# The MLP's pool of inner halves moves from the right side of SBUF to the left

## The chip, the cores and the metric

The kernel runs on one core of a Trainium2 chip. The metric is device time in microseconds (us), from the start of the program to the end of its last instruction; every time below is of that kind. A core has five engines that work side by side and are held together by semaphores: TensorE (PE, matrix products), VectorE (DVE), ScalarE (ACT), GpSimd (POOL) and SyncE (SP, which here issues most loads). SBUF is the on-chip memory of 128 partitions, and all addresses below are bytes in one partition.

## The reference, cut to what matters

The function is an encoder trunk of two layers over a sequence of 512 with 1024 channels. Each layer is a mixer and an MLP, both behind a norm whose shift, scale and gate come from the conditioning vector c. Layer 0 mixes with convolution and retention, layer 1 with S5 and a GLU:

```python
for layer in range(DEPTH):
    mod = (c_act @ ada_w[layer] + ada_b[layer])[:, None, :]
    shift_m, scale_m, gate_m, shift_f, scale_f, gate_f = jnp.split(mod, 6, axis=-1)
    h = _rmsnorm(x, norm_g[layer, 0]) * (1.0 + scale_m) + shift_m
    ...
    x = x + gate_m * mix
    h = _rmsnorm(x, norm_g[layer, 1]) * (1.0 + scale_f) + shift_f
    x = x + gate_f * (jnp.square(jax.nn.relu(h @ w_fc1[layer])) @ w_fc2[layer])
return _rmsnorm(x, norm_f)
```

## The kernel before

Activations lie with channels on partitions, as eight tiles of 128x512. Every large product is computed in three matmuls: an operand is split into a high part (a cast on ScalarE) and a low part (a subtraction on VectorE), and hi*hi, hi*lo and lo*hi are added up in PSUM (`mm3`). A weight unit of 128x1024 is loaded into a `raw` tile (7 slots, shared by all streams of weights, those of the modulation included), cast to `wh` (L197) and subtracted to `wl` (L192). A unit is then eight times three matmuls of 128x512 into one PSUM tile.

The program runs through `mixer0`, `mlp(0)`, `s5` (which ends with the GLU), `mlp(1)` and the final norm. At the end of `mixer0` the eight output units of `w_out` give the new x tiles (L719), their squares are summed (L284 on VectorE), the first inputs `fh` and `fl` of the MLP are formed (L753, L754), and background work runs beside it: `silu_c` loads c into `cb` and applies silu (L420, L421), and `ada_dve` computes four modulation columns on VectorE from loaded `raw<-adt` units (L436, sixteen of them). Then `mlp(0)` starts on the not yet normalised inputs with two fc1 units (`wl_2200` and `wl_2204` are their low parts) and applies the norm's factor later; `raw<-fc` are the MLP's weights, `ident,rr` is the broadcast of that factor.

Beside `mlp(0)`, VectorE and GpSimd build the matrices of S5 and write them to DRAM. At the entry to `s5` the first of them are loaded back in this order: `wi`, `cs`, then a GLU weight (`raw<-w_ga`), `tt`, `e`, and again `wi`, `cs`, `tt`, `e` for the second block.

Tiles come from pools. Pools of the left side of SBUF are stacked upwards, pools of the right side downwards from the top (229344). The pool `fp` holds the MLP's inner halves: eight slots of `fh` and eight of `fl`, 2048 bytes each, 32768 in all. It is opened by `open_fp` at the end of `mixer0` and again at the end of `s5`, and closed after each MLP. A tile that is put where another lay waits until the last reader or writer of the old one is done.

The scheduler arranges the instructions of each engine itself, from its own estimate of when operands and places come free; matmuls of some stretches and all loads of SyncE (`load`, L175) are kept in the order of the program.

Of the kernel before, what the change touches and what calls it, by code (L numbers as in the profile page):

```python
# [135 lines left out]
class Kern:  # L136
# [602 lines left out]

    def open_fp(self):  # L740
        self.fp = self.stack.enter_context(
            self.tc.tile_pool(name="fp", bufs=8, side="right", reuse_waits="tile"))


    def pre(self, l, i):
# [959 lines left out]
```

## Time and profile before

| what | value |
|---|---|
| three runs | 1225.39, 1228.76, 1229.54 us |
| their median | 1228.76 us |
| the profiled execution | 1225.63 us, of which the span is 1223.9 us |
| mean granted TensorE clock | 0.985 |
| busy share of the span | PE 96%, DVE 71%, ACT 39% |

The span runs from the first to the last instruction in the trace; the rest of the profiled execution's time (1.7 us) lies around it. Shares are means over all stages. At the ends of the stages VectorE or a load can be what the next instruction waits for.

### The profile page before, as it was taken

The numbers are of one execution on the slowest core, as the hardware profiler recorded it, in microseconds if no ns is written. First come the engines' busy times: TensorE is split into PE (matmuls) and PEld (weight loads), VectorE is DVE, ScalarE is ACT, GpSimd is POOL, SyncE is SP. The second block draws the span as 40 slices with busy tenths as digits, with TensorE's granted clock in tenths as the row PEclk, the third lists the DMA queues.
The fourth block names the chain that finished last, engine by engine and source line by source line (L and its number), as shares of the span: only waits on it lengthen the run. The fifth ranks groups of instructions, "written<-read, shape, count | busy, mean of one in ns | idle before, by whom it ended". The sixth has DMA issues, their size and how long they took to land.

```text
span 1223.9 us, 17714 instructions
## 1 busy us (share of the span) xinstructions
PE 1175.5 (96%) x6830; PEld 932.9 (76%) x6830; DVE 873.4 (71%) x1605; ACT 475.9 (39%) x752; POOL 109.4 (9%) x223
## 2 busy tenths in 40 slices
PE   6999999999999999999989888999999999999996
PEld 5777756776878878878767677788888888888885
DVE  6899995899998799798968999498552332332343
ACT  4423313455523423423424674344551532422530
POOL 0000000100011223344422100000000000000000
PEclk9999999999999999999999898999999999999998
DMA  9755341635356689889798877376343332333201
GB/s 354 259 172 184 132 170 35 213 118 189 104 159 233 212 285 290 262 282 277 216 337 291 310 265 284 121 244 212 147 138 103 88 102 86 103 90 100 69 1 69
DMA packets 65700, 223.59 MB, mean 183 GB/s; under 512 B 11168, under 2 KB 11552, under 8 KB 63568
## 3 DMA queue, kind: packets, MB, share of 16 engines
q1 hardware_dynamic: 48528, 174.63, 42.0%
q0 software_dynamic: 16512, 46.79, 12.5%
q8 instruction: 53, 0.87, 0.3%
q10 hardware_dynamic: 576, 1.05, 0.2%
q14 instruction: 31, 0.25, 0.1%
HBM read 197.77 MB, written 29.82 MB: 186 GB/s over the span
## 4 chain that ended last, share of the span: by engine, by line
PE 83%; DVE 8%; DMA 5%; ACT 2%; issue 1%; SPq 0%; DVEq 0%; ACTq 0%
PE ps L170 83%; DVE wk L1296 2%; DMA wk<-k_chan 1%; DMA raw<-adn 1%; DVE xt L1428 1%; DMA raw<-adt 1%; DVE xt L1427 1%; PE ps L1252 1%; DVE wl L192 0%; DMA raw<-fc 0%; DMA x<-x 0%; DVE hx L1296 0%; DVE wk L1684 0%; ACT wh L197 0%; DVE sr L1296 0%
## 5 line engine op out<-in xcount | busy, mean ns | idle before, releaser
L197 ACT CAST wh<-raw 128x1024 fp32r<-128x1024 f32 x169 | 176.6, 1050 | 515.1 <-PE ps L170 452.7
L192 DVE TENSOR_TENSOR wl<-raw,wh 128x1024 fp32r<-128x1024 f32 x169 | 205.9, 1222 | 179.1 <-ACT wh L197 177.3
L170 PE MATMUL ps<-hh,wh 128*128 128x512 f32 x808 | 317.5, 399 | 4.6 <-ACT cm L789 2.2
L170 PE MATMUL ps<-hl,wh 128*128 128x512 f32 x808 | 317.1, 393 | 1.6 <-DVE hl L238 1.2
L170 PE MATMUL ps<-hh,wl 128*128 128x512 f32 x808 | 316.3, 392 | 0.8 <-DVE wl L192 0.8
L170 PE MATMUL ps<-fl,wh 128*128 128x512 f32 x544 | 215.9, 398 | 1.4 <-DVE fl L811 1.4
L170 PE MATMUL ps<-fh,wh 128*128 128x512 f32 x544 | 216.9, 400 | 0.0
L170 PE MATMUL ps<-fh,wl 128*128 128x512 f32 x544 | 216.0, 398 | 0.0
L170 PEld LDWEIGHTS ps<-hh,wh 128*128 128x128 f32 x808 | 152.4, 189 | 43.7 <-ACT wh L197 3.5
L170 PEld LDWEIGHTS ps<-hh,wl 128*128 128x128 f32 x808 | 152.7, 189 | 33.8 <-DVE wl L192 1.2
L170 PEld LDWEIGHTS ps<-hl,wh 128*128 128x128 f32 x808 | 152.8, 189 | 33.6 <-DVE hl L238 1.6
L170 PEld LDWEIGHTS ps<-fl,wh 128*128 128x128 f32 x544 | 102.9, 189 | 26.1 <-DVE fl L811 1.9
L170 PEld LDWEIGHTS ps<-fh,wh 128*128 128x128 f32 x544 | 102.8, 189 | 25.2 <-issue 0.8
L170 PEld LDWEIGHTS ps<-fh,wl 128*128 128x128 f32 x544 | 102.7, 189 | 24.8
L538 DVE SCALAR_TENSOR_TENSOR cacc<-apad,cvw,cacc 128x512 f32<-128x512 f32 x120 | 83.6, 744 | 0.0
L827 DVE SCALAR_TENSOR_TENSOR x<-ps,mod,x 128x512 f32<-128x512 f32 x40 | 29.9, 748 | 68.2 <-PE ps L170 68.1
L811 DVE TENSOR_TENSOR fl<-wk,fh 128x512 fp32r<-128x512 f32 x64 | 44.0, 688 | 18.1 <-ACT fh L810 18.1
L862 DVE TENSOR_TENSOR w<-pb,bt 128x512 f32<-128x512 f32 x64 | 41.4, 686 | 5.0 <-DMA bt<-bt 2.8
L280 ACT ACTIVATE wk<-x 128x512 f32<-128x512 f32 x35 | 22.1, 631 | 58.2 <-DVE x L827 32.7
L807 ACT ACTIVATE wk<-wk 128x512 f32<-128x512 f32 x64 | 40.7, 636 | 1.5
L810 ACT CAST fh<-wk 128x512 fp32r<-128x512 f32 x64 | 39.8, 622 | 1.7
L436 DVE SCALAR_TENSOR_TENSOR raw<-raw,x 128x512 f32<-128x512 f32 x52 | 33.2, 686 | 9.2 <-DMA raw<-adt 6.8
(245 smaller groups left out, 1285.8 us busy)
## 6 DMA issues: line engine op xcount, KB each, us to landing
raw<-fc SPq DMA_DIRECT2D x128, 512.0 KB, 4.3
raw<-adn SPq DMA_DIRECT2D x50, 512.0 KB, 4.9
raw<-adt SPq DMA_DIRECT2D x34, 512.0 KB, 4.9
pb<-d_pw POOLq DMA_DIRECT2D x32, 256.0 KB, 8.5
bt<-bt POOLq DMA_DIRECT2D x16, 512.0 KB, 9.6
d_e<-eb POOLq DMA_DIRECT2D x16, 512.0 KB, 4.7
d_wi<-eb POOLq DMA_DIRECT2D x16, 512.0 KB, 7.8
wi<-d_wi SPq DMA_DIRECT2D x8, 1024.0 KB, 5.7
```

The source lines that it names most:

```text
L170: i = self.nc.tensor.matmul(out, lhsT=lhsT, rhs=rhs, start=start, stop=stop, **kw)
L192: self.keep(self.nc.vector.tensor_tensor(lo, raw, hi.bitcast(F32), SUB))
L197: self.keep(self.nc.scalar.copy(hi, raw))
L280: nc.scalar.activation(sq, t, AF.Square)
L436: self.keep(nc.vector.scalar_tensor_tensor(half, half, 1.0, self.cb[k], MUL, MUL, accum_out=v[:, 2 * k + h:2 * k + h + 1]))
L538: nc.vector.scalar_tensor_tensor(ac, ap[:, t:t + S], cvw[:, i * TAPS + t:i * TAPS + t + 1], ac, MUL, ADD)
L807: nc.scalar.activation(f, r, AF.Square)
L810: nc.scalar.copy(hi, f)
L811: nc.vector.tensor_tensor(lo, f, hi.bitcast(F32), SUB)
L827: nc.vector.scalar_tensor_tensor(self.x[m], ps, gate[:, m:m + 1], self.x[m], MUL, ADD)
L862: V.tensor_tensor(o, x, y, op)
L1296: pin(nc.vector.tensor_tensor(*args))
```

## The change

The pool `fp` is allocated from the left side.

```diff
     def open_fp(self):
         self.fp = self.stack.enter_context(
-            self.tc.tile_pool(name="fp", bufs=8, side="right", reuse_waits="tile"))
+            self.tc.tile_pool(name="fp", bufs=8, reuse_waits="tile"))
```

Before, `fp` lay at 196576 to 229344, above everything else; after, it lies at 155104 to 187872, directly on the pools that live all the time, and the pools that are opened after it (`cb`, and `pl` for the work beside the MLP) start at 187872 instead of 155104 and end at 229344. In `s5`, which opens its pool when `fp` is closed, both slots of `wi` (155104 to 171488) and those of `cs` and `tt` then lie where the MLP's `fh` and `fl` were, and `e` lies where the background work was; before, these four lay on the background work and the second slot of `e` on `fh`.

The program's operations are the same, but the scheduler arranges the end of `mixer0` otherwise. VectorE, at the first new x tile (`x_1945`), before: all sixteen L436 of the modulation (on `raw_1975` to `raw_2067`) stand ahead of it.

```order
L438 TENSOR_TENSOR rv_2070<-rv_2070 128x2
L382 TENSOR_TENSOR mod_123<-rv_2070,adab_122 128x2
L719 SCALAR_TENSOR_TENSOR x_1945<-ps_1790,mod_123,x_104 128x64x8
L719 SCALAR_TENSOR_TENSOR x_1966<-ps_1791,mod_123,x_106 128x64x8
L866 TENSOR_SCALAR s1_2416<-s8_2423 128x64
L719 SCALAR_TENSOR_TENSOR x_1979<-ps_1792,mod_123,x_108 128x64x8
L192 TENSOR_TENSOR wl_1782<-raw_1772,wh_1780 128x1024
L719 SCALAR_TENSOR_TENSOR x_1999<-ps_1793,mod_123,x_110 128x64x8
L866 TENSOR_SCALAR s2_2417<-s1_2416 128x64
L192 TENSOR_TENSOR wl_1788<-raw_1778,wh_1786 128x1024
L192 TENSOR_TENSOR wl_2023<-raw_1784,wh_2021 128x1024
L754 SCALAR_TENSOR_TENSOR fl_1950<-x_1945,gs_124,fh_1949 128x512
```

The same place after the change:

```order
L436 SCALAR_TENSOR_TENSOR raw_1995,rv_2008<-raw_1995,cb0_1956 128x512
L436 SCALAR_TENSOR_TENSOR raw_1995,rv_2008<-raw_1995,cb1_1957 128x512
L719 SCALAR_TENSOR_TENSOR x_1945<-ps_1790,mod_123,x_104 128x64x8
L436 SCALAR_TENSOR_TENSOR raw_1996,rv_2008<-raw_1996,cb0_1956 128x512
L719 SCALAR_TENSOR_TENSOR x_1966<-ps_1791,mod_123,x_106 128x64x8
L436 SCALAR_TENSOR_TENSOR raw_1996,rv_2008<-raw_1996,cb1_1957 128x512
L866 TENSOR_SCALAR s1_2416<-s8_2423 128x64
L192 TENSOR_TENSOR wl_1782<-raw_1772,wh_1780 128x1024
L719 SCALAR_TENSOR_TENSOR x_1979<-ps_1792,mod_123,x_108 128x64x8
L192 TENSOR_TENSOR wl_1788<-raw_1778,wh_1786 128x1024
L436 SCALAR_TENSOR_TENSOR raw_2015,rv_2059<-raw_2015,cb0_1956 128x512
L436 SCALAR_TENSOR_TENSOR raw_2015,rv_2059<-raw_2015,cb1_1957 128x512
```

Six L436 stand ahead of `x_1945` now, and ten come after it, between the x tiles and the low parts of the units. The multiplications of the retention's gates (L704) and `cb` have changed places as well: the gates are first, so `cb` and the modulation start later.

VectorE, some twenty rows further on, at the low part `wl_2200` of the first fc1 unit, before:

```order
L284 TENSOR_TENSOR ssq_1947<-ssq_1947,wk_1968 128x512
L754 SCALAR_TENSOR_TENSOR fl_1972<-x_1966,gs_124,fh_1971 128x512
L754 SCALAR_TENSOR_TENSOR fl_1985<-x_1979,gs_124,fh_1984 128x512
L870 SCALAR_TENSOR_TENSOR s1_2416<-s2_2417,s1_2416 128x64
L754 SCALAR_TENSOR_TENSOR fl_2005<-x_1999,gs_124,fh_2004 128x512
L719 SCALAR_TENSOR_TENSOR x_2050<-ps_2025,mod_123,x_112 128x64x8
L284 TENSOR_TENSOR ssq_1947<-ssq_1947,wk_1981 128x512
L192 TENSOR_TENSOR wl_2200<-raw_2194,wh_2198 128x1024
L870 SCALAR_TENSOR_TENSOR s1_2416<-s2_2417,s1_2416 128x64
```

After:

```order
L719 SCALAR_TENSOR_TENSOR x_2148<-ps_2123,mod_123,x_116 128x64x8
L438 TENSOR_TENSOR rv_2070<-rv_2070 128x2
L870 SCALAR_TENSOR_TENSOR s1_2416<-s2_2417,s1_2416 128x64
L284 TENSOR_TENSOR ssq_1947<-ssq_1947,wk_2052 128x512
L382 TENSOR_TENSOR mod_123<-rv_2070,adab_122 128x2
L866 TENSOR_SCALAR s3_2418<-s1_2416 128x64
L866 TENSOR_SCALAR s2_2417<-s2_2417 128x64
L284 TENSOR_TENSOR ssq_1947<-ssq_1947,wk_2116 128x512
L192 TENSOR_TENSOR wl_2200<-raw_2194,wh_2198 128x1024
```

Before, `wl_2200` came right after the fifth x tile (`x_2050`) and the second sum of squares (L284); now the seventh x tile (`x_2148`) and the fifth sum of squares stand ahead of it. From `x_1945` up to and with `wl_2200` VectorE has, after the change, 46 instructions: 7 L719, 10 L436, 5 L192, 6 L754, 5 L284 and 13 small ones of 64 columns or fewer. The slot of `raw` into which the first fc1 unit is loaded comes free with `wl_1788` before and with `wl_2087` after (the row 349 of VectorE, 21 of the 46); that of the second with `wl_2023` before and after with the second L436 on `raw_2066` (30 of the 46). TensorE takes the last products of the four open output units one unit after the other instead of all four high parts first, so that three matmuls fewer stand ahead of the end of the first; and it takes nineteen matmuls of the first fc1 unit before the second unit's first, where it took three.

SyncE, at the entry to `s5`, with the semaphores that each load waits for, before:

```order
L177 DMA wi_6051<-d_wi_132 128x2048 [waits DMASW7_49,DMASW5_49,DVE_49]
L177 DMA cs_6053<-d_tab_129 128x1024 [waits DMASW4_49,DMASW5_49,DMASW3_49,DMASW6_49,DMASW2_49,DMASW7_49,DMASW1_49,DMAHW1_49,DMASW0_49,Pool_49]
L177 DMA raw_6055<-w_ga 128x1024 [waits DMAHW5_49,DMAHW2_49,Activation_49]
L177 DMA tt_6057<-d_t_134 128x1024 [waits DMASW7_49,DMAHW3_49,DMASW0_49,Pool_49]
L177 DMA e_6059<-d_e_131 128x2048 [waits DMASW3_49,DMASW4_49,DMASW2_49,DMASW7_49,DMASW1_49,DMAHW4_49,DMASW0_49,PE_49]
```

After:

```order
L177 DMA wi_6051<-d_wi_132 128x2048 [waits DMASW5_49,DMASW7_49,PE_49,Pool_49]
L177 DMA cs_6053<-d_tab_129 128x1024 [waits DMAHW1_49,DMASW4_49]
L177 DMA raw_6055<-w_ga 128x1024 [waits DMAHW5_49,DMAHW2_49,DVE_49]
L177 DMA tt_6057<-d_t_134 128x1024 [waits DMASW5_49,DMASW6_49,DMASW3_49,DMASW7_49,DMASW2_49,DMAHW3_49,DMASW1_49,DMASW0_49]
L177 DMA e_6059<-d_e_131 128x2048 [waits DMAHW4_49,DVE_49]
```

The order is the same. `wi` waits for a matmul now (PE_49) where it waited for VectorE, and the semaphore's value is that of the last matmul of `mlp(0)`, which reads `fh_5575` and `wl_5897`; `e` waits for VectorE where it waited for that matmul. The loads in between have no wait for TensorE, but stand behind `wi` in SyncE's order. From there to the end the order of every engine is unchanged.

## Rows read from the trace of the kernel before

**Rows 1.** The page of the profile: busy time of each engine, and the chain by line.

```profile
PE 1175.5 (96%) x6830; PEld 932.9 (76%) x6830; DVE 873.4 (71%) x1605; ACT 475.9 (39%) x752; POOL 109.4 (9%) x223
...
PE ps L170 83%; DVE wk L1296 2%; DMA wk<-k_chan 1%; DMA raw<-adn 1%; DVE xt L1428 1%; DMA raw<-adt 1%; DVE xt L1427 1%; PE ps L1252 1%; DVE wl L192 0%; DMA raw<-fc 0%; DMA x<-x 0%; DVE hx L1296 0%; DVE wk L1684 0%; ACT wh L197 0%; DVE sr L1296 0%
```

**Rows 2.** VectorE's timeline, 226 to 260 us (start, duration, operation, idle before).

```profile
226.70 0.68 DVE L436 SCALAR_TENSOR_TENSOR raw<-raw,cb 128x512 f32<-128x512 f32 x1
...
227.31 0.69 DVE L436 SCALAR_TENSOR_TENSOR raw<-raw,cb 128x512 f32<-128x512 f32 x1
...
244.21 2.13 DVE L719 SCALAR_TENSOR_TENSOR x<-ps,mod,x 128x512 f32<-128x512 f32 x2 [1.73 <-PE ps L170]
...
247.22 1.22 DVE L192 TENSOR_TENSOR wl<-raw,wh 128x1024 fp32r<-128x1024 f32 x1
...
254.20 1.41 DVE L754 SCALAR_TENSOR_TENSOR fl<-x,gs,fh 128x512 fp32r<-128x512 f32 x2
255.53 0.22 DVE L870 SCALAR_TENSOR_TENSOR s<-s,s 128x64 f32<-128x64 f32 x1
...
256.32 1.14 DVE L719 SCALAR_TENSOR_TENSOR x<-ps,mod,x 128x512 f32<-128x512 f32 x1
257.30 0.68 DVE L284 TENSOR_TENSOR ssq<-ssq,wk 128x512 f32<-128x512 f32 x1
257.90 1.21 DVE L192 TENSOR_TENSOR wl<-raw,wh 128x1024 fp32r<-128x1024 f32 x1
259.03 0.22 DVE L870 SCALAR_TENSOR_TENSOR s<-s,s 128x64 f32<-128x64 f32 x1
```

**Rows 3.** TensorE's timeline at the same place: first unit, first MLP matmuls, broadcast.

```profile
248.50 0.50 PE L170 MATMUL ps<-hh,wl 128*128 128x512 f32 x1 [0.78 <-DVE wl L192]
...
269.02 0.40 PE L170 MATMUL ps<-fh,wh 128*128 128x512 f32 x1
...
269.48 0.39 PE L170 MATMUL ps<-fh,wl 128*128 128x512 f32 x1
...
282.04 1.05 PE L170 MATMUL ps<-ident,rr 128*128 128x128 f32 x8
```

**Rows 4.** Loads into raw tiles, 215 to 300 us: time to landing.

```profile
DMA to landing us min/median/max: 3.6/4.5/9.1
```

**Rows 5.** SyncE's timeline, 640 to 680 us: the S5 loads.

```profile
658.20 0.33 SPq L177 DMA_DIRECT2D wi<-d_wi  x1
...
659.33 0.36 SPq L177 DMA_DIRECT2D raw<-w_ga  x1
```

**Rows 6.** Timelines of TensorE, ScalarE and VectorE at the entry to S5.

```profile
663.78 0.40 PE L170 MATMUL ps<-fh,wl 128*128 128x512 f32 x1
...
671.39 3.51 PE L170 MATMUL ps<-hl,wi 128*64 128x64 f32 x64 [0.46 <-DVE hl L1296]
...
684.30 0.44 PE L170 MATMUL ps<-tt,hl 128*64 128x128 f32 x4
...
669.00 1.05 ACT L197 CAST wh<-raw 128x1024 fp32r<-128x1024 f32 x1
...
672.05 1.22 DVE L192 TENSOR_TENSOR wl<-raw,wh 128x1024 fp32r<-128x1024 f32 x1
...
674.94 1.29 DVE L1296 TENSOR_TENSOR wk<-ps,cs 128x512 f32<-128x512 f32 x2 [0.42 <-PE ps L170]
```

**Rows 7.** Landings of all wi loads; then of w_ga alone, issued at 659.33.

```profile
DMA to landing us min/median/max: 4.7/5.7/11.1
...
DMA to landing us min/median/max: 8.9/8.9/8.9
```

**Rows 8.** Stretches: PE, PEld, DVE, ACT, POOL busy; clock, DMA share, GB/s.

```profile
664.00:760.00 96.00, 80.40 (x1113) 65.96 (x1113) 92.08 (x138) 61.87 (x162) 5.60 (x10) 0.93 0.84 313
...
668.00:670.00 2.00, 0.97 (x18) 0.46 (x8) 1.81 (x8) 1.51 (x4) 0.79 (x2) 1.00 1.08 440
```

**Rows 9.** Busy time in the stretch after the k_chan load is awaited.

```profile
605.00:640.00 35.00, 30.47 (x197) 23.63 (x196) 23.63 (x43) 8.95 (x13) 9.38 (x18) 0.97 0.97 327
```

## The prediction, made before the changed kernel ran

> **What bounds the kernel now.** I read the page first: TensorE is busy for 96% of the span, and in the chain its matmuls hold 83%, with small shares for VectorE (S5's products, L1296) and for a load of `k_chan` [rows 1]. So a change that moves only places and waits can show only where TensorE waits now, or where the change makes it wait. Two such places are touched, and I read them from the timelines. At the end of `mixer0` TensorE waits 0.78 us for the low part `wl_1782` of an output unit before the matmul at 248.50, then has no gap worth a row up to the first MLP matmul at 269.02 [rows 3]. VectorE feeds it there: it sits idle for 1.73 us until `x_1945` can start at 244.21, and works without a gap from there [rows 2]. At the entry to S5 the roles turn: from 664 to 760 us VectorE is busy for 92.08 of 96 us and TensorE for 80.40 [rows 8], so there whatever delays VectorE delays the end.
>
> **The change part by part: the end of the mixer.** The reader has seen that ten L436 are moved from VectorE's idle time ahead of `x_1945` to the loaded stretch behind it, and that `wl_2200`, which the third MLP matmul needs, is now the 46th instruction from `x_1945`. I price the 46 by the distance from one start to the next: L719 0.98 (256.32 to 257.30), L284 0.60 (to 257.90), L192 1.13 (to 259.03), L436 0.61 (226.70 to 227.31), L754 0.665 (two in the 1.33 from 254.20 to 255.53), and a small one 0.125 (255.53 to 256.32 holds one and an L754) [rows 2]. That is 7 x 0.98 + 10 x 0.61 + 5 x 1.13 + 6 x 0.665 + 5 x 0.60 + 13 x 0.125 = 27.2 us.
>
> The start: three matmuls of some 0.23 us fewer (269.02 to 269.48 holds two [rows 3]) stand ahead of the first x tile, so `x_1945` starts at 244.21 - 0.68 = 243.53. `wl_2200` is then done at 270.8, and its matmul can start 0.06 later (as 248.50 follows the end of `wl_1782`, 247.22 + 1.22 = 248.44 [rows 2, 3]), at 270.9.
>
> When does TensorE come to it? The six instructions up to `wl_1782` take 2 x 0.98 + 2 x 0.61 + 0.125 + 1.22 = 4.5 us, so it is done at 248.06 and TensorE goes on at 248.12, 0.38 us earlier than before. The work from there is the same, so the third MLP matmul is reached at 269.48 - 0.38 = 269.10 [rows 3]. It waits 1.8 us, and against before it starts 1.4 us late. Nothing behind it gives that back: in the 13 us from 269.02 to the broadcast at 282.04 [rows 3] TensorE is the bound, and the MLP behind goes on by TensorE. **Term: +1.4 us.** Bounds: if VectorE gains 1.8 us on this count, there is no wait and -0.4 us remains; if each instruction took its whole duration, with no overlap (7 x 1.14 + 10 x 0.69 + 5 x 1.21 + 6 x 0.705 + 5 x 0.68 + 13 x 0.22 = 31.4 us [rows 2]), `wl_2200` would come at 275.0, +5.5 us. The starts in a row show the overlap, so I take the first count.
>
> The loads are moved too. The load of the first fc1 unit waited for the second low part after `x_1945`; now its slot comes free after 21 of the 46, by the same distances 15.1 us, at 258.7. It lands 4.5 us later by the median, 9.1 by the slowest here [rows 4], at 263.2 or 267.8, and with the cast (1.05 us, as the one at 669.00 [rows 6]) at 268.9 at the latest. `wl_2200` starts at about 269.6, so VectorE's queue covers it; without that cover it would cost what it comes late. The second unit's load comes free after 30 of the 46, at 263.4, and lands at 267.9 to 272.5; TensorE wants its high part only after nineteen matmuls of the first unit (some 4.2 us), at 274.8. Both are priced at nothing.
>
> **The entry to S5.** `wi` was issued at 658.20, under the MLP's last matmuls [rows 5]; now it waits for the last of them, which starts at 663.78 and takes 0.40 [rows 6]: 664.2, 6.0 us later. Behind it on SyncE stand `cs`, `w_ga`, `tt` and `e`. `wi` itself lands 4.7 to 5.7 us after its issue (fastest and median of eight [rows 7]), 668.9 to 669.9, and TensorE needs it at 671.39 [rows 6], when its other operand comes: no cost, unless it takes the longest landing of the eight, 11.1.
>
> `w_ga` has less room. It was issued 1.13 us after `wi` and landed 8.9 us later, at 668.2 [rows 5, 7]; the cast was at 669.00, and VectorE took the low part at 672.05 [rows 6]. Now it is issued at 665.3. Upper bound of its landing: the same 8.9 us, 674.2. Lower bound: `wi` at its fastest, 668.9, and then the 1 MB of `cs` and `w_ga` at the 440 GB/s that the queues move at 668 us [rows 8], 2.4 us: 671.3. I take 672.3, nearer the lower bound, since the loads before had to share with the background's last writes. With the cast, VectorE starts `wl` at 673.4 instead of 672.05, 1.3 us late, and 0.42 us of that lies in its later wait for TensorE, ahead of 674.94 [rows 6]. **Term: +0.9 us**, with bounds of 0 (a landing at 671.3 makes it 0.3 late, which that wait takes up) and +2.8 (674.2). What waits behind the instruction at 672.05 is VectorE's whole queue of S5, and TensorE with it.
>
> The Trainium skill, "DMA: Bandwidth & Descriptors", section "Rules for kernel authors", says to issue a DMA early, compute, and wait for its semaphore late. This trace agrees: `w_ga` landed at 668.2, 0.8 us ahead of its cast, only because it left before the MLP's end. The rule speaks against the change, which puts the issue at that end.
>
> `tt` is not wanted before 684.30 [rows 6]: issued half a us behind `w_ga`, at 665.8, it is there by 676.9 even with the longest landing of rows 7, 11.1; `e` and the second block's loads are wanted later still. At MLP 1 the second `fp` finds its place free. All are priced at nothing.
>
> **The sum.** 1.4 + 0.9 = +2.3 us. The profiled execution took 1225.63 us, so it would be 1227.9. That execution is 3.1 us below the median of the three runs, 1228.76; I put the base midway, 1227.2, and predict 1229.5 us. A measurement of this kernel tells some 0.3%, 3.7 us, from no change; so the forecast is: a small loss that reads as no change.
>
> **The rivals.**
> *A, slower: S5's entry pays in full.* `w_ga` keeps its 8.9 us, the loads behind it now being issued together with it: +2.8, sum +4.2, 1231.4 us. It passes 0.3% if `w_ga` lands after 673.7. For it: that the queues are full at 440 GB/s [rows 8]; against: less background traffic. Chance 0.18.
> *B, slower: VectorE's queue ahead of `wl_2200` slips* towards its whole durations: +5.5 + 0.9, 1233.6 us. It decides from a `wl_2200` ready after 272.3. Against it: the measured starts. Chance 0.07.
> *C, faster: the wait for `k_chan`.* From 605 to 640 us TensorE is busy for 30.47 of 35 us [rows 9], behind a load that MLP 0's background awaits. The shift of TensorE against the background could shorten it; all of it back would be -4.5 + 2.3, 1225.0 us, and with both terms at their lower ends 1222.3. Against it: that chain's order is unchanged. Chance 0.11.
> *D, nothing.* VectorE catches up and `w_ga` lands by 671.3: 1226.8 to 1227.2 us. For it: the lower bounds. Chance 0.16. The same page of the Trainium skill, section "Anatomy of one DMA", gives 2.0 us and the bytes by 436 GB/s; as an estimate the 2 MB up to `w_ga` would be there at 671.0, which goes with this rival.
> My forecast has 0.48.
>
> **Range and chances.** Taking off half of C below and half of B above, and with the 1.5 us by which the base is uncertain, 1223.0 to 1235.5 us; the likeliest case alone, 1227 to 1232. Faster by over 0.3%: only C at its lower end or with a low base, 0.10. Slower: B, most of A, and a little of the forecast, 0.25. Within 0.3%: 0.65.
>
> **What would show it.** First, a TensorE wait of one to two us for VectorE (L192) at the third MLP matmul, near 270, and the broadcast near 283.4; a wait under 0.3 us there makes the first term wrong. Second, `wi` issued right after the MLP's last matmul, `w_ga` landing near 672 to 673 measured from a last matmul at 664 (both shifted by the first term), and VectorE's `wl` waiting for ScalarE's cast; if `wl` waits for nothing, the second term is 0. Third, no change in the time from there to the end. The prediction is wrong if a stretch that neither place touches changes by more than 2 us, above all 605 to 640, or if `wi` itself holds TensorE.

## The result, and the profile after

The changed kernel took 1235.01 us (median of 10 runs, 1231.22 to 1244.67) against 1227.57 us before on the same chip (10 runs, 1223.51 to 1229.54): a ratio of 1.0071, 95% interval 1.0046 to 1.0096. It is slower by 0.7%. 1229.5 us had been predicted, within 1223.0 to 1235.5, and "no change" as the likeliest reading.

The page of the profile after (span 1231.3 us, profiled execution 1233.1 us), first the busy times, then the chain of waits by line:

```profile
PE 1175.3 (95%) x6830; PEld 933.5 (76%) x6830; DVE 873.5 (71%) x1605; ACT 475.8 (39%) x752; POOL 109.5 (9%) x223
...
PE ps L170 83%; DMA raw<-fc 2%; DMA raw<-adn 1%; DMA raw<-adt 1%; DMA wi<-d_wi 1%; DVE wl L192 1%; PE ps L1252 1%; DMA hh<-adn 1%; DVE raw L436 1%; DVE x L719 0%; DVE w L862 0%; DMA x<-x 0%; PE ps L1341 0%; DVE wk L1684 0%; ACT tu L1363 0%
```

The busy times are those of before [rows 1] within 0.2 us for each engine (TensorE's weight loads within 0.6); the span is 7.4 us longer. So no engine has more to do, and TensorE stands idle for 7.6 us more (1231.3 - 1175.3 us against 1223.9 - 1175.5). Sums over the whole span do not tell where. I looked for it by comparing when the same event comes in both traces.

**The end of the mixer.** VectorE's timeline after (start, duration, operation, idle time before it and what ended it):

```profile
228.68 0.69 DVE L704 TENSOR_TENSOR g<-g,ps 128x512 f32<-128x512 f32 x1 [7.32 <-PE ps L170]
...
235.29 0.69 DVE L421 TENSOR_TENSOR cb<-cb,wk 128x512 f32<-128x512 f32 x1 [1.25 <-ACT wk L420]
...
242.96 1.17 DVE L719 SCALAR_TENSOR_TENSOR x<-ps,mod,x 128x512 f32<-128x512 f32 x1 [2.21 <-PE ps L170]
```

The first row is the one to look at. VectorE sits idle for 7.32 us until the first gate's product comes from TensorE. Before, `cb` and the L436 [rows 2] filled this time; now the gates (L704) stand first in VectorE's order and `cb` behind them, though its load was there. The stretch 216 to 245 us (busy times of PE, PEld, DVE, ACT, POOL; granted clock, DMA share, GB/s), before and after:

```profile
216.00:245.00 29.00, 27.43 (x151) 22.80 (x144) 25.08 (x70) 11.30 (x18) 3.10 (x10) 1.00 0.72 228
...
216.00:245.00 29.00, 27.85 (x133) 23.22 (x133) 17.71 (x43) 10.46 (x15) 0.00 (x0) 0.94 0.31 113
```

VectorE sits idle for 7.4 us more (11.29 against 3.92). Not all of it is the order's: in this profile TensorE's granted clock was 0.91 from 209.00 to 227.59 us, between two of its broadcasts, where it was 1.00 before, and TensorE took 1.6 us longer there. The run with less background (below) keeps the changed order and had the clock at 1.00 there; in it VectorE is idle for 9.7 us. What the order leaves over is work: from the first L669 (212.25 before, 210.09 after) to `x_1945` VectorE is busy for 28.04 us before and 21.57 after, so 6.5 us, the ten L436 above all, are not yet done. Then TensorE's timeline. Before, the stretch begins with this broadcast:

```profile
228.16 3.73 PE L170 MATMUL ps<-ident,rr 128*128 128x128 f32 x32
```

And after:

```profile
227.59 3.73 PE L170 MATMUL ps<-ident,rr 128*128 128x128 f32 x32
...
269.95 0.50 PE L170 MATMUL ps<-fh,wl 128*128 128x512 f32 x1 [1.22 <-DVE wl L192]
...
282.60 1.05 PE L170 MATMUL ps<-ident,rr 128*128 128x128 f32 x8
```

This answers to [rows 3]: the third MLP matmul waits for VectorE. Counted from the broadcast at 228.16 or 227.59, `x_1945` comes 0.68 us earlier (15.37 us behind it instead of 16.05), the third matmul 1.0 us later (42.36 instead of 41.32) and the MLP's broadcast 1.1 us later; in the trace's own time that broadcast comes 0.56 us later than before. From there TensorE catches up: at 348 us it is 0.3 us ahead of before.

**Eighty us later.** TensorE's timeline in the middle of MLP 0, where the background of S5 has its transposes (L1089, of the phases `wd`). First before, where TensorE comes to them without a wait:

```profile
360.66 1.03 PE L1089 MATMUL ps<-ident,wd 128*128 128x128 f32 x8
361.45 0.48 PE L170 MATMUL ps<-fh,wh 128*128 128x512 f32 x1
361.76 0.40 PE L170 MATMUL ps<-fl,wh 128*128 128x512 f32 x1
362.00 0.40 PE L170 MATMUL ps<-fh,wl 128*128 128x512 f32 x1
362.23 0.39 PE L170 MATMUL ps<-fh,wh 128*128 128x512 f32 x1
```

And after:

```profile
362.68 1.12 PE L1089 MATMUL ps<-ident,wd 128*128 128x128 f32 x4 [2.19 <-DVE wd L874]
365.04 1.12 PE L1089 MATMUL ps<-ident,wd 128*128 128x128 f32 x4 [1.24 <-DVE wd L874]
...
366.81 0.63 PE L170 MATMUL ps<-fh,wl 128*128 128x512 f32 x1
367.24 0.63 PE L170 MATMUL ps<-fh,wh 128*128 128x512 f32 x1
```

Two things are to be read. TensorE waits 2.19 + 1.24 = 3.43 us for VectorE's copies of the phases (L874). And the matmuls behind the wait start 0.43 us apart (366.81 to 367.24), where they start some 0.235 apart before (362.00 to 362.23). VectorE's timeline says why. The last copies before:

```profile
354.98 1.93 DVE L874 COPY wd<-wd 64x512 f32<-64x512 f32 x3
```

And after:

```profile
363.80 1.19 DVE L874 COPY wd<-wd 64x512 f32<-64x512 f32 x2
```

They end at 356.9 and at 365.0, which is 74.9 and 82.4 us after the broadcast, 7.5 us later. From the broadcast to the last copy, before and after (columns as above):

```profile
282.04:356.91 74.87, 72.26 (x397) 56.63 (x396) 69.97 (x203) 37.47 (x56) 0.00 (x0) 1.00 0.48 162
...
282.60:364.99 82.39, 76.82 (x417) 60.26 (x415) 76.66 (x234) 38.40 (x57) 0.00 (x0) 0.98 0.47 154
```

So 6.7 of the 7.5 us are work of VectorE: what is left of the work not done at the mixer's end, and two low parts of weights more (15 L192 instead of 13, 2.6 us), which TensorE's units want before the late copies are done. Before, TensorE came to the transposes 3.8 us behind the last copy (360.66 against 356.9); that was all the slack there was. The stretch 360 to 370 us (columns as above), before:

```profile
360.00:370.00 10.00, 10.00 (x49) 8.16 (x48) 7.77 (x11) 3.07 (x4) 6.30 (x12) 1.00 0.71 238
```

And after:

```profile
360.00:370.00 10.00, 6.57 (x22) 4.90 (x21) 9.70 (x18) 2.22 (x3) 2.18 (x4) 0.66 0.30 96
```

The granted clock is 0.66 of full speed after the wait, 1.00 before: part of the stretch ran at 1.2 GHz and not at 2.4. Between 348 and 384 us TensorE goes from 0.3 us ahead to 5.9 us late: 6.2 us, of which 3.4 are the wait and 2.8 the lower clock. It stays 5.9 us late up to 505 us.

**The rest.** Near 524 and 530 us TensorE waits 1.66 and 1.08 us for `fl` (L811), where the first profile of before shows one wait of 0.77: 2.2 us with what lies around them. The end of MLP 0 comes 7.95 us late. At the entry to S5 three timelines answer to [rows 5, 6]. SyncE's:

```profile
672.22 0.33 SPq L177 DMA_DIRECT2D wi<-d_wi  x1
```

ScalarE's:

```profile
680.37 1.04 ACT L197 CAST wh<-raw 128x1024 fp32r<-128x1024 f32 x1 [3.31 <-DMA raw<-w_ga]
```

And VectorE's:

```profile
681.45 1.23 DVE L192 TENSOR_TENSOR wl<-raw,wh 128x1024 fp32r<-128x1024 f32 x1 [1.36 <-ACT wh L197]
```

`wi` is issued 0.09 us after the end of the MLP's last matmul (671.74 + 0.39), ScalarE waits for `w_ga`, and VectorE for ScalarE. The first scan of S5 starts 8.84 us later than before, 0.89 more than MLP 0's end. Behind it TensorE waits for the second block's `wi`, for which it does not wait before:

```profile
689.26 3.02 PE L170 MATMUL ps<-hl,wi 128*64 128x64 f32 x64 [3.90 <-DMA wi<-d_wi]
```

That wait costs nothing here, since VectorE works on: all 32 scans come between 8.84 and 8.86 us late. At the end of S5 1.4 us come back: before, TensorE ran at a granted clock of 0.83 from 760 to 770 us; after, the same part of the program (768 to 778 us) ran at 1.00. From the end of S5 to the end of the program both traces take 438.55 us. The end is 7.4 us late: -0.3 + 6.2 + 2.2 - 0.2 + 0.9 - 1.4.

### The profile page after: what moved, and what is told of

Its sections match the earlier page's. It is cut to its first block, busy times and chain, and to the rows that moved or that the text cites. A ratio compares the mean times of both kernels' runs of the same rounds, so it can differ in the third digit from the quotient of the medians.

```text
span 1231.3 us, 17715 instructions
## 1 busy us (share of the span) xinstructions
PE 1175.3 (95%) x6830; PEld 933.5 (76%) x6830; DVE 873.5 (71%) x1605; ACT 475.8 (39%) x752; POOL 109.5 (9%) x223
## 4 chain that ended last, share of the span: by engine, by line
PE 84%; DMA 7%; DVE 5%; ACT 2%; issue 2%; SPq 0%; DVEq 0%; ACTq 0%
PE ps L170 83%; DMA raw<-fc 2%; DMA raw<-adn 1%; DMA raw<-adt 1%; DMA wi<-d_wi 1%; DVE wl L192 1%; PE ps L1252 1%; DMA hh<-adn 1%; DVE raw L436 1%; DVE x L719 0%; DVE w L862 0%; DMA x<-x 0%; PE ps L1341 0%; DVE wk L1684 0%; ACT tu L1363 0%
## 5 line engine op out<-in xcount | busy, mean ns | idle before, releaser
L192 DVE TENSOR_TENSOR wl<-raw,wh 128x1024 fp32r<-128x1024 f32 x169 | 206.1, 1221 | 178.7 <-ACT wh L197 176.7
L811 DVE TENSOR_TENSOR fl<-wk,fh 128x512 fp32r<-128x512 f32 x64 | 43.9, 688 | 19.7 <-ACT fh L810 19.7
L436 DVE SCALAR_TENSOR_TENSOR raw<-raw,x 128x512 f32<-128x512 f32 x52 | 33.3, 686 | 11.8 <-DMA raw<-adt 11.8
```

The costliest lines, as they stand in the source:

```text
L192: self.keep(self.nc.vector.tensor_tensor(lo, raw, hi.bitcast(F32), SUB))
L436: self.keep(nc.vector.scalar_tensor_tensor(half, half, 1.0, self.cb[k], MUL, MUL, accum_out=v[:, 2 * k + h:2 * k + h + 1]))
L811: nc.vector.tensor_tensor(lo, f, hi.bitcast(F32), SUB)
```

## The experiments

Theory one: the order at the mixer's end costs VectorE idle time, and this comes out as a wait at L1089 and a low clock behind it. Rivals: the new places as such (S5's loads, MLP 1); and, theory two, that the lateness of the background meets TensorE anywhere, L1089 being only the first place. Ratios are against the kernel before on the same chip, with their 95% intervals.

**Only layer 1 on the left.** `fp` stays right for MLP 0 and goes left for MLP 1.

```diff
-            self.open_fp()
+            self.open_fp(side="right")
...
```

(`open_fp` hands the side on to the pool.)

> The pool is left on the right side for layer 0's MLP and goes to the left only for layer 1's; the order of TensorE, VectorE and SyncE is that of before. If the loss comes from what the pool's place in layer 0 does to the order at the end of the mixer (and to the S5 loads), the time is that of before within 0.3%, and no wait over 0.5 us stands at the phase transposes (L1089). If the place of the pool itself is slow (its addresses, read by the MLP's matmuls), layer 1's MLP takes about as much longer as layer 0's did, and some 3 to 4 us of the 7.4 show here.

Measured: 1225.82 us, ratio 0.9995 (0.9980 to 1.0011); no wait at L1089. The place in MLP 1 costs nothing that shows.

**Only the order at the mixer's end.** The kernel before, `fp` on the right, with a gap that puts `cb` at 187872, where it lies after the change.

```diff
-                    cb = dp.enter_context(tc.tile_pool(name="cb", bufs=1, reuse_waits="tile"))
+                    cb = dp.enter_context(tc.tile_pool(name="cb", bufs=1, reuse_waits="tile")); cb.tile([P, 8192], F32, name="gap")
```

> The kernel before, with the MLP's pool on the right, and only the pool of c moved up by 32768 bytes, to 187872, where the change put it; S5's loads keep their places. The scheduler then puts the gates ahead of c and ten L436 behind the first x tile, as after the change. If the order is the cause, VectorE is idle for some 10 us between 221 and 244, the phase copies come 7 to 8 us later, TensorE waits 2 to 4 us at L1089, and the time is 1232 to 1236 us, with wi issued under the MLP's last matmuls as before. If the loss lies in S5's loads or in the pool's place, the time is that of before, 1226 to 1229.

Measured: 1238.1 us, ratio 1.0080 (1.0047 to 1.0112). VectorE's timeline:

```profile
230.10 0.69 DVE L704 TENSOR_TENSOR g<-g,ps 128x512 f32<-128x512 f32 x1 [5.72 <-PE ps L170]
```

TensorE's:

```profile
367.20 2.35 PE L1089 MATMUL ps<-ident,wd 128*128 128x128 f32 x8 [5.46 <-DVE wd L874]
```

The stretches there, columns as above:

```profile
360.00:370.00 10.00, 4.42 (x18) 3.25 (x17) 9.44 (x20) 2.04 (x3) 0.00 (x0) 0.83 0.28 93
370.00:380.00 10.00, 10.00 (x37) 7.93 (x37) 9.70 (x15) 1.23 (x2) 6.46 (x12) 0.82 0.44 159
```

The gap alone gives the idle time, the wait and a loss as large as the change's, while the way from MLP 0's end to the first scan stays at 13.45 us (13.33 before, 14.22 after). So it is the order that the scheduler makes when `cb` lies there, and neither `fp`'s side itself nor, but for its 0.9 us, S5. This order is not in every row that of the change: the third MLP matmul does not wait here, and the wait at L1089 is longer.

**The transposes one block later**, on the changed kernel, to take TensorE's wait away and leave VectorE's lateness.

```diff
-                if b == 0:
+                if b == 1:
                     turns()
```

> The changed kernel, with the transposes of the phases (L1089) put one table block later in the program (a block is 2.4 us or more of VectorE's work), so that TensorE comes to them later. If VectorE's backlog meets TensorE there, the wait of 3.4 us and the low clock behind it go for the most part, and the time falls by 3 to 6 us, to 1229 to 1232. If the later wait at 524 to 530 us is a consequence of the same backlog, it goes or stays independently of this, and is read from the trace: under 1.0 us if TensorE's delay at L1089 was its cause, 2 to 3 us if VectorE's backlog or the loads were. If the order at the mixer's end costs by itself, the time stays at 1235.

Measured: 1237.46 us, ratio 1.0077 (1.0051 to 1.0103). The wait at L1089 is gone, and nothing is gained. TensorE's timeline shows what came in its place (the granted clock was 0.83 from 420 to 430 us):

```profile
422.65 0.50 PE L170 MATMUL ps<-fh,wh 128*128 128x512 f32 x1 [1.62 <-ACT wh L197]
423.91 0.51 PE L170 MATMUL ps<-fh,wl 128*128 128x512 f32 x1 [0.52 <-DVE wl L192]
...
647.29 0.66 PE L1252 MATMUL ps<-eb,bp 128*32 128x128 f32 x8 [2.85 <-DVE eb L862]
```

From the broadcast to the end of MLP 0 it takes 391.85 us (after: 389.37, before: 381.98). This speaks for theory two: to move one meeting point does not remove the lateness.

**The GLU's weight first**, on the changed kernel: `w_ga` is issued ahead of `wi`.

```diff
+            self.glu.ahead(4, 3)
             load(0, "wi", "cs")
...
-            self.glu.ahead(4, 3)
```

> The changed kernel, with the GLU weight w_ga loaded ahead of wi and cs at the entry to S5, so that it doesn't stand behind the load that waits for the MLP's last matmul. By the theory of the prediction VectorE's low part no longer waits for the cast, and the first scan starts 0.9 us earlier against the MLP's last matmul (13.3 us behind it, as before, instead of 14.2). If the end of S5 is set by VectorE, the total falls by 0.9 us; if by TensorE's clock in the last blocks, it does not move by more than 0.5. In no case does it give back the 6 to 8 us that arise ahead of S5.

Measured: 1235.35 us, ratio 1.0083 (1.0057 to 1.0109); from MLP 0's end to the first scan 14.21 us (14.22 without the edit). The load came early (issued at 660.49), but then its cast stands ahead of the norm's L258 in ScalarE's timeline:

```profile
677.68 1.03 ACT L197 CAST wh<-raw 128x1024 fp32r<-128x1024 f32 x1
678.62 0.20 ACT L258 ACTIVATE rt<-rv 128x4 f32<-128x4 f32 x1
```

VectorE then waits 1.43 us for `rt`, 0.95 more than after the change alone (0.48), and after that no more for the cast (1.36 there). One wait was changed into another.

**Doses of VectorE work at the mixer's end**, on the kernel before: five or ten multiplications of 128x512 (0.69 us each) on a work tile, in its old order.

```diff
             ts(lr, lr, -1e-4, None, ALU.min)
+            nc.vector.memset(w1, 0.0)
+            for _ in range(5):
+                V.tensor_tensor(w1, w1, w1, MUL)
```

> The kernel before, with VectorE given a memset and five more multiplications of 128x512 (0.60 us each, some 3.3 us in all) on a scratch tile that the phases' computation writes later; they lie between the x tiles at the end of the mixer, ahead of the phases, and the output does not depend on them. Theory one, a slack at the transposes: before the change the phase copies are ready 3.8 us ahead of TensorE (356.9 against 360.66), so this dose causes no wait at L1089 and the time is that of before within 0.3%. Theory two, the work beside the MLP is itself the longest path up to S5 (TensorE waits for its end, 2.44 and 1.50 us at 636 to 638): whatever delays it comes through one for one, here +3 us, as a longer wait at 636 or at an earlier place.

> The same with ten multiplications, 6.3 us in all, about the VectorE time that the change loses ahead of the first x tile. Theory one: a wait of some 2.5 us at L1089 with 2 us of low clock behind it, +4 to +5 us. Theory two: +6 us, wherever TensorE meets it. If neither holds and the loss is from the loads that the change moves later, the time stays within 0.3% of before.

Measured: 1228.74 us, ratio 1.0026 (1.0009 to 1.0043), and 1229.74 us, ratio 1.0031 (1.0014 to 1.0049). TensorE's timeline with five:

```profile
360.38 0.66 PE L1092 MATMUL ps<-ident,wd 128*128 128x128 f32 x4 [0.61 <-DVE wd L874]
```

With ten:

```profile
363.52 0.66 PE L1092 MATMUL ps<-ident,wd 128*128 128x128 f32 x4 [1.34 <-DVE wd L874]
365.88 0.66 PE L1092 MATMUL ps<-ident,wd 128*128 128x128 f32 x4 [1.70 <-DVE wd L874]
```

The last copy ends 79.9 and 82.4 us after the broadcast (74.9 without a dose): work at the mixer's end does come out at L1089, once it is more than the slack. Ten make the copies as late as the change does (the ten and their memset are 7.5 us of work). But the ratio is less than half the change's. The stretch with ten tells a part of the difference:

```profile
360.00:370.00 10.00, 6.96 (x34) 5.28 (x33) 9.73 (x19) 2.22 (x3) 1.64 (x3) 1.00 0.42 132
```

With waits of 3.04 us in sum the granted clock stayed at 1.00. Matched matmul by matmul, TensorE loses 3.5 us from 360 to 374 us (in the time of the trace before), where the change loses 6.2.

**`k_chan` earlier**, on the kernel before and on the changed one, for the rival in which the wait near 605 to 640 us moves.

```diff
+            if q == 3 and l == 0:
+                next(bg)
```

(and in that generator the load of `k_chan` is its first step).

> The kernel before, with the load of k_chan issued one quarter of the MLP earlier, ahead of eight loads of 256 KB behind which it took 17 us. VectorE's wait of 9.15 us at 628 goes, and with it TensorE's waits of 2.44 and 1.50 us at 636 to 638 and the low clock behind them: 3 to 5 us faster, 1221 to 1224 us, if nothing else holds the end of the work beside the MLP. If a later load or the writes of that work hold it, under 2 us.

> The changed kernel with the same earlier load. Its waits at 644 to 646 (2.45 and 1.50 us) go in the same way, 3 to 5 us. If the loss of the change sits at L1089 and at 524 to 530, those waits stay and the distance to the same kernel with the pool on the right stays 7 to 9 us. If the end of the work beside the MLP is what counts, the distance shrinks to below 4 us, since VectorE then has 9 us of room before S5.

Measured: 1224.99 us, ratio 0.9991 (0.9975 to 1.0007), and 1236.39 us, ratio 1.0101 (1.0057 to 1.0145). VectorE's 9.15 us of waiting for `k_chan` are gone, and in their place VectorE's timeline of the kernel before with the edit has:

```profile
629.60 1.23 DVE L192 TENSOR_TENSOR wl<-raw,wh 128x1024 fp32r<-128x1024 f32 x1 [10.45 <-ACT wh L197]
```

The next weight is loaded late too. TensorE's waits behind it (2.91 + 1.50 us near 637) do not shrink, and the change's waits at L1089 stay as they were.

**Less background.** Between the broadcast and the transposes four copies (64x512, 0.61 us each) go to GpSimd, and twelve VectorE instructions of complex products are left out, some 7.5 us in all. S5's matrices are then not the reference's. On the changed kernel and, as a control, on the one before.

```diff
...
-            cmul(fpr, fpi, pr[:, 1:9], pi[:, 1:9], br, bi, q1, q2)
+            tt(fpr, pr[:, 1:9], br)
+            tt(fpi, pi[:, 1:9], bi)
...
-                cp(t[0:64], src[0:64, 0:8].rearrange("p m g -> p g m"))
+                nc.gpsimd.tensor_copy(t[0:64], src[0:64, 0:8].rearrange("p m g -> p g m"))
...
```

(the second copy and the products of 256 columns in the same way).

> The changed kernel with some 7.5 us of work less on VectorE between the broadcast and the transposes L1089: four copies of 64x512 (0.61 each) go to GpSimd, four of the six instructions of the 512-column product and of each of the two 256-column products are left out (four of 0.61 and eight of 0.34). The places of the transposes in TensorE's order stay; the matrices of S5 are not those of the reference any more. Theory one (the idle time that VectorE lost at the mixer's end comes out as TensorE's wait at L1089 and the low clock behind it): the last phase copy is back near 75 us after the broadcast, no wait at L1089, full clock there, broadcast to the end of MLP 0 at 382 to 384.5 us, ratio 1.000 to 1.003. Theory two (the loss only moves on to later waits, as when the transposes were put later): the wait at L1089 is gone but 390 us remain, ratio 1.006 to 1.009.

> The same work taken from the kernel before, as a control. Theory one: TensorE did not wait at L1089, 3.8 us of slack become 11, nothing is gained: ratio 0.998 to 1.001. Theory two, in the form that VectorE's total background load in MLP 0 sets the end of it: some of the 7.5 us comes back as shorter waits at 636 to 638, ratio 0.994 to 0.998.

Measured: 1231.04 us, ratio 1.0046 (1.0029 to 1.0064), and 1228.21 us, ratio 1.0016 (1.0001 to 1.0031). The edit freed more than meant: the last copy comes 57.6 us after the broadcast, not 75, since the scheduler also drew the copies forward. TensorE's timeline on the changed kernel:

```profile
361.44 1.03 PE L1094 MATMUL ps<-ident,wd 128*128 128x128 f32 x8
```

And the stretch:

```profile
360.00:370.00 10.00, 10.00 (x48) 8.18 (x47) 9.84 (x21) 3.17 (x4) 6.11 (x12) 1.00 0.65 211
```

No wait, full clock, and 380.85 us from the broadcast to the end of MLP 0: 8.5 us less than after, and 1.1 less than before. The first wait of the change, at the third MLP matmul (27.00 us after `x_1945`, 25.27 before), is still there. With the light background the change costs 0.30% (1.0046 against 1.0016; 2.8 us between the medians), where it cost 0.71% (7.4 us). That is the better part of the loss, though the two intervals still overlap a little, and the ratio of the changed kernel stays above the 1.000 to 1.003 that theory one had given. Its profiled execution (1227.39 us) is the fastest of its eight runs, so its profile does not show where the slower ones lose.

**Only the four copies on GpSimd**, on the changed kernel.

> The changed kernel with only the four copies of 64x512 moved from VectorE to GpSimd, which has nothing to do there; all results stay those of the reference. Theory one: the last phase copy comes 2.4 us earlier (80.0 after the broadcast), the two waits at L1089 fall from 3.4 us to about 1.0, the clock stays full, 3 to 6 us come back: ratio 1.002 to 1.005. Theory two: the loss moves on: 1.006 to 1.009. A third way: copies on GpSimd slow VectorE down while they run, and the copies come no earlier: 1.007 or more with the waits as they are.

Measured: 1235.89 us, ratio 1.0082 (1.0060 to 1.0105). GpSimd's timeline:

```profile
322.11 4.62 POOL L1076 COPY wori<-pr 64x512 f32<-64x512 f32 x1 [111.02 <-DVE s L862]
326.77 2.03 POOL L1077 COPY wori<-pr 64x512 f32<-64x512 f32 x1
```

TensorE's:

```profile
362.16 0.66 PE L1089 MATMUL ps<-ident,wd 128*128 128x128 f32 x4 [1.63 <-DVE wd L874]
363.40 0.66 PE L1089 MATMUL ps<-ident,wd 128*128 128x128 f32 x4 [0.58 <-DVE wd L874]
```

The waits fell to 2.21 us, not to 1.0: the last copy comes 81.1 us after the broadcast, 1.3 earlier, not 2.4. The third way of the expectation is a part of this. Beside the copies VectorE's own instructions took longer, as these two pairs of one kind show, the first while GpSimd copies and the second just after:

```profile
327.74 1.28 DVE L862 TENSOR_TENSOR s<-s 128x64 f32<-128x64 f32 x2
...
331.89 0.36 DVE L862 TENSOR_TENSOR s<-s 128x64 f32<-128x64 f32 x2
```

VectorE's busy time from the broadcast to the last copy fell by 0.9 us (75.76 against 76.66), though the four copies were 2.4. The clock stayed at 1.00 from 360 to 370, and at the matmul of 442 us before, counted from the broadcast, only 2.1 us are lost, where the change has 5.3. But at that of 535 us 5.5 us are lost (7.6 after the change), with a wait of 1.86 us for L811 and a granted clock of 0.83 from 520 to 530. The time does not show the gain.

**Both kernels profiled again**, unchanged, to see which waits come back.

> The changed kernel itself, profiled once more, to see which waits of its profile come back. Theory one: the waits at L1089 are set by the order and come back within 0.3 us (2.19 and 1.24), since VectorE works without a gap up to there; the low clock behind them comes back too. The wait for L811 near 524 to 530 us (2.74 together) follows VectorE's waits for loads and comes back with another size, anywhere from 0.8 to 3. Theory two, that all of these vary from run to run: the sum at L1089 differs by more than 1 us.

> The kernel before, profiled once more. Theory one: no wait at L1089 again (3.8 us of slack), full clock from 355 to 380; the wait for L811 near 522 us, 0.77 in the first profile, comes back with 0.8 to 3, so that the 2.2 us by which the two first profiles differ there are not the change's. Theory two: it stays below 1 us, and the 2.2 us are the change's.

Measured, one execution each: 1235.23 and 1226.56 us (a second execution of the kernel before on that chip took 1230.60). The changed kernel's TensorE:

```profile
364.09 0.66 PE L1089 MATMUL ps<-ident,wd 128*128 128x128 f32 x4 [2.20 <-DVE wd L874]
366.45 1.11 PE L1089 MATMUL ps<-ident,wd 128*128 128x128 f32 x4 [1.70 <-DVE wd L874]
```

Its stretches there:

```profile
360.00:370.00 10.00, 6.10 (x24) 4.56 (x23) 9.74 (x19) 2.22 (x3) 1.26 (x3) 0.75 0.27 101
370.00:380.00 10.00, 10.00 (x41) 8.00 (x40) 7.67 (x11) 1.05 (x1) 5.23 (x10) 0.91 0.52 168
```

The waits (3.90 us) and the low clock come back; counted from the broadcast, TensorE goes from 1.0 to 7.8 us late there. Matched matmul by matmul, the profiles with the changed order and its transposes in their place lose 6.2 us (after), 6.8 (again), 5.9 (GLU's weight first) and 6.2 (`k_chan` early) from 360 to 374 us of the trace before; those with the order of before (before, again, only layer 1, `k_chan` early) lose nothing there. The kernel before again has no wait at L1089, and the clock is 1.00 from 355 to 380. Near 522 to 531 us the changed kernel waits 1.21 + 1.09 = 2.3 us and the one before 1.08. In other profiles with the order of before these waits are 1.70 (only layer 1) and 2.96 (less background). They vary too much to say how much of the 2.2 us is the change's.

## Why the prediction was wrong

**The two terms came about as described.** *The end of the mixer, +1.4 us:* 1.0 us, counted from the broadcast at 228.16 or 227.59. `x_1945` came 0.68 us earlier against it, as forecast, the 46 instructions behind it took 26.9 us instead of 27.2, and the wait for `wl_2200` was in its place with 1.22 us (1.8 forecast). The profile after ran 0.57 us ahead at 227.59, so the MLP's broadcast came at 282.60, not at 283.4. But "nothing behind it gives that back" was wrong of TensorE too: by 348 us it had made up 0.9 of the 1.1 us. *The entry to S5, +0.9 us:* 0.89 us up to the first scan (0.6 to 1.5 in the other profiles in which the change's S5 loads were left as they are). `w_ga` had been put 8.5 us behind the start of the MLP's last matmul (672.3 against 663.78); ScalarE's wait for it ended at 680.37, 8.6 behind 671.74. The Trainium skill's "DMA: Bandwidth & Descriptors", section "Anatomy of one DMA", from which the prediction had estimated 671.0, so 7.2 us behind, fits its figures to single DMAs on the GpSimd path; for these loads from SyncE the estimate was 1.4 us short. What was priced at nothing at these places (`wi` itself, `tt`, `e`, the fc1 loads, MLP 1) shows no cost in the trace after. One sign of being wrong did come, that `wi` holds TensorE: the second block's did for 3.90 us (4.60 when profiled again), which the prediction had not seen; in the first of these profiles it cost nothing, as VectorE was the bound there.

**The step that failed** is the pricing of the moved L436. It said that "ten L436 are moved from VectorE's idle time ahead of `x_1945` to the loaded stretch behind it", and then only the 46 instructions up to `wl_2200` were counted. "Nothing behind it gives that back: ... TensorE is the bound, and the MLP behind goes on by TensorE" asked whether TensorE makes up its 1.4 us, and not whether VectorE makes up its own. VectorE came to `x_1945` with 6.5 us of work less done. Behind the broadcast it has no time to catch up in: from 283 to 362 us it is busy for 73.3 of 79 us. So everything behind was late, down to the phase copies 80 us on, 7.5 us late, where TensorE had 3.8 us of slack: it lost 6.2 us there, in waits and at the lower clock, and the prediction's sum has nothing for it. The order showed that the gates and `cb` had changed places and that the modulation starts later; the prediction set no price on it.

The runs show this cause in these parts: the order alone brings the loss (the gap below `cb`, 1.0080) and the other places do not (only layer 1, 0.9995); VectorE work put at the mixer's end comes out as a wait at L1089 beyond the slack (0.61 and 3.04 us); with the background lightened the wait and the low clock are gone, and the difference between the orders falls from 7.4 to 2.8 us. How much of these 2.8 us is the two terms', of which TensorE had made up most of the first, is not shown. What they do not support is that L1089 is the only place: with the wait moved away (1.0077) or cut by 1.2 us (1.0082) the time did not fall, and other waits and low clocks came later.

**The range and the rivals.** The measured 1235.0 us lies just inside the range, by luck: its upper end, 1235.5, was made of half of rival B. B ("VectorE's queue slips", 1233.6 us) came near in time, but by another mechanism: it looked at the queue ahead of `wl_2200`. C did not come: the waits at 636 to 646 us are 2.44 + 1.50 before and 2.45 + 1.50 after, and the run with `k_chan` early shows why there was nothing to win, as another load stands right behind. A and D concerned the two terms, which came out near the forecast. The text had named what would make it wrong: a stretch that neither place touches changing by more than 2 us. It had looked for that above all at 605 to 640; it was 360 to 370.

**What stays open:** why ten multiplications, with the copies as late as the change makes them, cost only 1.0031. In the one profile their waits left the clock at 1.00 (2.7 us less lost there), and they do not touch S5 (0.9 us less), which together is about the difference; whether the clock stays up in their other runs was not tried. Open too is why the time did not fall when the wait at L1089 was moved or cut, where the changed kernel with less background loses in its slower runs, and how much of the waits near 524 is the change's. No version was found that beats the kernel before.

## What to carry to other kernels

Idle time of an engine that is not the bound is not free when that engine has a backlog: if a change takes such time away, follow that engine's queue to the next place where the bounding engine waits for it, however far, and compare its lateness with the slack there (here 7.5 us against 3.8 us, 80 us later). Allocation alone can do this, as the run with the gap shows: the place of a tile decides what its first writer waits for and so how a scheduler orders its neighbours. And a wait on the bounding engine can cost more than its length: price it with the clock behind it, as a bound.

## What was not expected of the hardware

TensorE's clock after a wait. Behind 3.43 us of waits (2.19 + 1.24) the granted clock was 0.66 from 360 to 370 us, behind 3.90 (2.20 + 1.70) it was 0.75 and then 0.91, behind a single one of 5.46 it was 0.83 and 0.82, with `k_chan` early behind 3.43 (2.19 + 1.24) 0.66, with the GLU's weight first behind 3.89 (2.19 + 1.70) 0.83 from 365 to 375; matmuls started 0.43 us apart instead of 0.235. Behind 3.04 us (1.34 + 1.70) and 2.21 (1.63 + 0.58) it was 1.00. But with the four copies on GpSimd a single wait of 1.86 us near 522 us came with 0.83 from 520 to 530, so the length of the waits alone does not tell it. And the same copy of 64x512 that took VectorE 0.61 us took GpSimd 4.62, 2.03, 1.15 and 1.49 us while VectorE was at work beside it, and VectorE was slowed too: two operations of 64 columns took 1.28 us instead of 0.36.
